# Reciprocal square roots of all norms: a logarithm and an exponential on ScalarE with one Newton step, in place of an integer shift with three

## The chip, the cores and the metric

The kernel runs on one core of one Trainium2 chip. The metric is the time of one execution on the device in microseconds (us), the median of several runs. In the profile PE is TensorE (matmul, PEld its weight loads), DVE is VectorE, ACT is ScalarE, POOL is GpSimd and SP the engine that issues most of the DMA transfers. Every engine works through its own queue of instructions in order, and waits on semaphores for the others.

## The reference

One decoder layer on 1024 tokens of width 1024, all in float32:

```python
x = layer_norm(x, ln_in_g, ln_in_b)
mix = hybrid_mixer(x, ...)        # 8 forgetting-attention heads, 4 HGRN2 heads
x = layer_norm(ALPHA * x + mix, ln_mix_g, ln_mix_b)
ffn = peer_ffn(x, ...)            # top-16 of 128^2 experts, 8 heads
x = layer_norm(ALPHA * x + ffn, ln_ffn_g, ln_ffn_b)
# layer_norm:     (x - mu) * rsqrt(var + 1e-5) * g + b        (over 1024 columns)
# head_rms_norm:   x * rsqrt(mean(x * x) + 1e-6) * g          (each head, in the mixer)
```

Both kinds of norm need a reciprocal square root of one number for each token (layer norm) or for each token and head (RMS norm of the mixer's outputs).

## The kernel before, in words

Tokens lie on the 128 partitions, in blocks of 128. The layer runs over three groups of tokens: 256, 512 and 256 (`GROUPS`). Each group goes through the input projection (`project_cols`), the mixer (`fox` and `hgrn`, two generators whose steps alternate), the output projection with the second layer norm (`mix_out`), the selection of experts (`select`, `select_tail`) and then the experts: four token blocks by gathering rows of the two tables (`gather_u`, `gather_v`, on POOL's DMA queue with the arithmetic on DVE or PE), the other four as a dense product with the whole tables (`dense`). Gathers and the building of the dense weights (`gbuild`) are cut into small pieces, which `tick` deals out between the steps of the other stages at hand-set rates. Only the pieces marked by `pin` keep the program's order; the rest of an engine's queue is put in order by the framework's scheduler, which works with its own estimates.

`rsqrt` (L221) is called in five places, 32 times in all, each time on a tile of 128 partitions and one to eight columns:

- `ln` (L250) from `first_ln`: four calls of two token blocks each, in the first projection.
- `hgrn` (L613): eight calls with four columns, one for each token block. What waits for the result is the scaling on ACT (L615), then POOL (L616) and the transposes on PE (L620).
- `fox` (L720): twelve calls with four or eight columns, one for each pair of heads in each group. What waits is the scaling on DVE (L722) and then the transposes (L727).
- `ln` from `mix_out`: three calls, one for each group, before the transposes L270 into the selection.
- `ln` from `finish`: four calls with one column, when a gathered block is done; and `finish_dense` (L1195), one call at the very end.

ACT is also the engine that evaluates Exp, Ln, Sigmoid, Silu and Gelu, and before some of these its queue holds an instruction `ACT_TABLE_LOAD`, which the compiler puts there. The softmax of `fox` (L679), the decays of `hgrn` (L514 to L550) and the copies of the transposed probabilities (L702) all run on ACT.

Of the kernel before, what the change touches and what calls it, by code (L numbers as in the profile page):

```python
# [12 lines left out]
I32 = mybir.dt.int32  # L13
U32 = mybir.dt.uint32
AF = mybir.ActivationFunctionType
ALU = mybir.AluOpType
# [4 lines left out]
P = 128  # L21
# [50 lines left out]
class Layer:  # L72
# [147 lines left out]

    def rsqrt(self, pool, x, n):  # L221
        V = self.nc.vector
        sh = pool.tile([P, n], U32, name="rssh", tag="rssh")
        y = pool.tile([P, n], F32, name="rsy", tag="rsy")
        t = pool.tile([P, n], F32, name="rst", tag="rst")
        V.tensor_scalar(sh, x.bitcast(U32), 1, None, op0=ALU.logical_shift_right)
        V.tensor_scalar(y.bitcast(I32), sh, -1.0, float(0x5F3759DF), op0=ALU.mult, op1=ALU.add)
        for _ in range(3):
            V.tensor_tensor(t, y, y, op=ALU.mult)
            V.scalar_tensor_tensor(t, t, -0.5, x, op0=ALU.mult, op1=ALU.mult)  # L230
            V.scalar_tensor_tensor(y, t, 1.5, y, op0=ALU.add, op1=ALU.mult)
        return y

    def ln_stats(self, st, n, x, halves=(0, 1)):
# [1067 lines left out]
```

## Time and profile before

| | |
|---|---|
| median of three runs | 3125.99 us (3123.66 to 3131.1) |
| the profiled execution | 3124.38 us, its span 3122.6 us |
| busy: PE, DVE, ACT, POOL | 2629.1, 2728.4, 1143.5, 1725.8 us |
| `ACT_TABLE_LOAD` on ACT | 29, each 1283 ns |

The span runs from the first instruction to the last; the execution is 1.8 us longer than the span. A row of a timeline gives the start, the duration, the engine, the line, the operation, output and inputs, and in brackets how long the engine had been idle and who ended that. Consecutive like instructions are merged (x2). A row of the waits gives the total, the number and the longest. By stage: the first group's mixer lies at about 90 to 200 us, the second's at 565 to 825, the third's at 1135 to 1270; the dense product with the remaining gathers takes from about 1500 to the end.

### The profile page before, as it was taken

Reading aid. Unit: us, or ns where it says so; the run is one execution under the profiler, and the core shown is the slowest. Engines: PE = TensorE matmul, PEld = TensorE weight load, DVE = VectorE, ACT = ScalarE, POOL = GpSimd, SP = SyncE. Lnnn points to the kernel's source line nnn. Section 1 sums busy time; section 2 is a strip of 40 time slices with the busy share of each in tenths; the row PEclk is TensorE's granted clock in tenths of the full one; section 3 lists DMA queues with packets and bytes.
Section 4 is the critical chain, followed back from the end, with each engine's and each line's share of the span. In section 5 each row is a group of like instructions: output and inputs, shape, how many; then the busy total and the mean of one; then the engine's idle time right before and its main releaser. Section 6 shows DMA issues by size and latency. Waiting matters only on the chain. (4 is left out here: it accounts for less than half of the span.)

```text
span 3122.6 us, 45664 instructions
## 1 busy us (share of the span) xinstructions
PE 2629.1 (84%) x16057; PEld 2161.1 (69%) x16057; DVE 2728.4 (87%) x5549; ACT 1143.5 (37%) x2028; POOL 1725.8 (55%) x1264
## 2 busy tenths in 40 slices
PE   7767799777779767767459899899999999999995
PEld 6767689656657445657347778787778877877874
DVE  8658766588769988989889899899999999999998
ACT  4733222455222433776523223232222323322321
POOL 2343477555756644654036666665467665656652
PEclk9879899888889889878779999999999999999997
DMA  7542599755968857663379999999999999999994
GB/s 272 191 143 81 195 353 318 224 157 169 336 247 297 282 192 268 221 232 149 149 243 366 333 380 359 350 362 367 345 362 371 380 379 357 356 375 337 371 338 159
DMA packets 338662, 887.13 MB, mean 284 GB/s; under 512 B 29912, under 2 KB 124136, under 8 KB 336000
## 3 DMA queue, kind: packets, MB, share of 16 engines
q0 software_dynamic: 147456, 536.94, 47.1%
q1 hardware_dynamic: 185200, 338.38, 31.1%
q10 hardware_dynamic: 5776, 8.90, 0.8%
q8 instruction: 126, 2.06, 0.3%
q14 instruction: 104, 0.85, 0.1%
HBM read 821.67 MB, written 62.42 MB: 283 GB/s over the span
## 5 line engine op out<-in xcount | busy, mean ns | idle before, releaser
L1090 POOL DMA_INDIRECT rows<-in_u,gsel x512 | 689.5, 1347 | 471.5 <-DVE rows L1109 291.7
L1090 POOL DMA_INDIRECT rows<-in_v,gsel x512 | 642.2, 1254 | 417.8 <-DVE ys L1134 261.2
L1109 DVE SCALAR_TENSOR_TENSOR rows<-rows,gx 128x1024 f32<-128x1024 f32 x512 | 633.2, 1285 | 37.9 <-DMA rows<-in_u,gsel 27.0
L1134 DVE SCALAR_TENSOR_TENSOR ys<-rows,sd,ys 128x1024 f32<-128x1024 f32 x381 | 489.7, 1285 | 0.6
L283 PE MATMUL psh<-dxh,uh 128*128 128x512 f32 x1024 | 402.8, 393 | 29.5 <-ACT uh L1016 16.5
L285 PE MATMUL psh<-dxh,ul 128*128 128x512 f32 x1024 | 401.0, 392 | 9.5 <-DVE ul L1017 9.4
L284 PE MATMUL psh<-dxl,uh 128*128 128x512 f32 x1024 | 400.5, 391 | 0.0
L284 PE MATMUL psf<-vl,hh 128*128 128x512 f32 x768 | 310.9, 405 | 44.0 <-DVE vl L1017 43.1
L1016 ACT ACTIVATE vh<-vr 128x512 fp32r<-128x512 f32 x256 | 161.8, 632 | 433.4 <-PE psv L285 402.7
L285 PE MATMUL psf<-vh,hl 128*128 128x512 f32 x768 | 305.8, 398 | 0.0
L283 PE MATMUL psf<-vh,hh 128*128 128x512 f32 x768 | 278.8, 395 | 9.3 <-DVE dy L1049 7.3
L1016 ACT ACTIVATE uh<-ur 128x1024 fp32r<-128x1024 f32 x128 | 136.0, 1062 | 406.2 <-PE psh L284 399.5
L283 PEld LDWEIGHTS psh<-dxh,uh 128*128 128x128 f32 x1024 | 193.5, 189 | 77.2 <-ACT hs L1030 20.5
L285 PEld LDWEIGHTS psh<-dxh,ul 128*128 128x128 f32 x1024 | 193.4, 189 | 50.5 <-DVE ul L1017 10.5
L210 ACT ACTIVATE whi<-wraw 128x1024 fp32r<-128x1024 f32 x130 | 136.5, 1056 | 241.9 <-PE psf L284 62.4
L213 POOL TENSOR_TENSOR wlo<-wraw,whi 128x1024 fp32r<-128x1024 f32 x70 | 172.8, 2474 | 91.7 <-ACT whi L210 89.2
L284 PEld LDWEIGHTS psh<-dxl,uh 128*128 128x128 f32 x1024 | 193.2, 189 | 39.5
L284 PEld LDWEIGHTS psf<-vl,hh 128*128 128x128 f32 x768 | 147.6, 192 | 91.4 <-DVE vl L1017 60.6
L1017 DVE TENSOR_TENSOR vl<-vr,vh 128x512 fp32r<-128x512 f32 x256 | 169.8, 685 | 12.4 <-ACT vh L1016 12.4
L283 PEld LDWEIGHTS psf<-vh,hh 128*128 128x128 f32 x768 | 145.4, 189 | 46.9 <-DVE dy L1049 9.6
L213 DVE TENSOR_TENSOR wlo<-wraw,whi 128x1024 fp32r<-128x1024 f32 x60 | 83.9, 1400 | 106.1 <-ACT whi L210 106.1
L285 PEld LDWEIGHTS psf<-vh,hl 128*128 128x128 f32 x768 | 148.1, 193 | 29.8
(338 smaller groups left out, 6510.4 us busy)
## 6 DMA issues: line engine op xcount, KB each, us to landing
ur<-in_ut SPq DMA_DIRECT2D x128, 512.0 KB
vr<-in_v SPq DMA_DIRECT2D x256, 256.0 KB
d_g<-slab SPq DMA_DIRECT2D x16, 2048.0 KB
gt<-d_g SPq DMA_DIRECT2D x32, 1024.0 KB
wraw<-in_wq SPq DMA_DIRECT2D x48, 512.0 KB
wraw<-in_wt SPq DMA_DIRECT2D x34, 512.0 KB
wraw<-in_wn SPq DMA_DIRECT2D x24, 512.0 KB
wraw<-in_wo SPq DMA_DIRECT2D x24, 512.0 KB
```

The lines of the kernel that those rows point to most:

```text
L210: nc.scalar.activation(hi, raw, AF.Copy)
L213: eng.tensor_tensor(lo, raw, hi.bitcast(F32), op=ALU.subtract)
L283: mm(out, lh, rh, start=start, stop=False, **kw)
L284: mm(out, lh, rl, start=False, stop=False, **kw)
L285: mm(out, ll, rh, start=False, stop=stop, **kw)
L1016: nc.scalar.activation(hi, raw, AF.Copy)
L1017: nc.vector.tensor_tensor(lo, raw, hi.bitcast(F32), op=ALU.subtract)
L1090: self.nc.gpsimd.indirect_dma_start(out=t, out_offset=None, in_=tab, in_offset=bass.IndirectOffsetOnAxis(ap=idx, axis=0))
L1109: self.pin(nc.vector.scalar_tensor_tensor(u, u, 1.0, x2, op0=ALU.mult, op1=ALU.mult, accum_out=sd[:, n : n + 1]), "u")
L1134: self.pin(nc.vector.scalar_tensor_tensor(ys, v, h, ys, op0=ALU.mult, op1=ALU.add), "w")
```

## The change

`rsqrt` takes its first estimate from ACT: the logarithm of x, written over by exp(-0.5 times it). One Newton step follows on DVE. Before, the estimate was made on DVE from the bits of x (a shift and a subtraction from a constant), and three Newton steps followed. The tile of the shift goes. The function has two lines less, so the lines of the kernel after it are lower by two in the changed kernel.

```diff
     def rsqrt(self, pool, x, n):
         V = self.nc.vector
-        sh = pool.tile([P, n], U32, name="rssh", tag="rssh")
         y = pool.tile([P, n], F32, name="rsy", tag="rsy")
         t = pool.tile([P, n], F32, name="rst", tag="rst")
-        V.tensor_scalar(sh, x.bitcast(U32), 1, None, op0=ALU.logical_shift_right)
-        V.tensor_scalar(y.bitcast(I32), sh, -1.0, float(0x5F3759DF), op0=ALU.mult, op1=ALU.add)
-        for _ in range(3):
-            V.tensor_tensor(t, y, y, op=ALU.mult)
-            V.scalar_tensor_tensor(t, t, -0.5, x, op0=ALU.mult, op1=ALU.mult)
-            V.scalar_tensor_tensor(y, t, 1.5, y, op0=ALU.add, op1=ALU.mult)
+        self.nc.scalar.activation(y, x, AF.Ln)
+        self.nc.scalar.activation(y, y, AF.Exp, scale=-0.5)
+        V.tensor_tensor(t, y, y, op=ALU.mult)
+        V.scalar_tensor_tensor(t, t, -0.5, x, op0=ALU.mult, op1=ALU.mult)
+        V.scalar_tensor_tensor(y, t, 1.5, y, op0=ALU.add, op1=ALU.mult)
         return y
```

In the changed kernel ACT's queue holds 92 table loads, 63 more than the 29 of before: 31 stand before a logarithm of `rsqrt` (L225) and 25 before its exponential (L226), the other seven are more before functions that were there already.

ACT's queue in the first group's mixer, where the first calls of `hgrn` and `fox` fall; `pr` are the softmax's exponentials, `pt` the transposed probabilities, E the decays, `ov` the scaling of HGRN2's output. Before:

```order
L550 ACTIVATE E<-E 128x512
L679 ACTIVATE pr,ls<-psf,nm 128x256
L702 ACTIVATE pt<-psf 128x256
L550 ACTIVATE E<-E 128x512
L702 ACTIVATE pt<-psf 128x128
L550 ACTIVATE E<-E 128x512
L679 ACTIVATE pr,ls<-psf,nm 128x128
L711 ACTIVATE o<-psv 128x2x64
L615 ACTIVATE ov<-ov,rsy 128x128 x4
```

The same place in the changed kernel:

```order
L225 ACT_TABLE_LOAD
L225 ACTIVATE rsy<-ms 128x4
L709 ACTIVATE o<-psv 128x2x64
L226 ACT_TABLE_LOAD
L226 ACTIVATE rsy<-rsy 128x4
L548 ACTIVATE E<-E 128x512
L677 ACTIVATE pr,ls<-psf,nm 128x256
L700 ACTIVATE pt<-psf 128x256
L225 ACT_TABLE_LOAD
L225 ACTIVATE rsy<-l_1622 128x4
L613 ACTIVATE ov<-ov,rsy 128x128
L226 ACT_TABLE_LOAD
```

Four table loads and four activations (the last Exp is the next row) now stand among the softmax, the decays and the copies.

ACT's queue in the dense product, where the second gathered block is finished (`rows` is its layer norm's scaling, `vh`, `uh` and `hh` the high parts of the tables' and the hidden tiles, `hs` the Gelu). Before:

```order
L1030 ACTIVATE hs<-psh 128x512
L1033 ACTIVATE hh<-hs 128x512
L1016 ACTIVATE vh<-vr 128x512 x2
L1016 ACTIVATE uh<-ur 128x1024
L1030 ACTIVATE hs<-psh 128x512
L259 ACTIVATE rows<-rows,lnnm,rsy 128x1024
```

The same place in the changed kernel:

```order
L1028 ACTIVATE hs<-psh 128x512
L1031 ACTIVATE hh<-hs 128x512
L225 ACT_TABLE_LOAD
L225 ACTIVATE rsy<-lnve 128x1
L1014 ACTIVATE vh<-vr 128x512
L226 ACT_TABLE_LOAD
L226 ACTIVATE rsy<-rsy 128x1
L1014 ACTIVATE vh<-vr 128x512
L257 ACTIVATE rows<-rows,lnnm,rsy 128x1024
L1014 ACTIVATE uh<-ur 128x1024
L1028 ACT_TABLE_LOAD
L1028 ACTIVATE hs<-psh 128x512
```

The logarithm and the exponential stand behind `hh` and one of them behind a `vh`, and the next Gelu has a table load of its own.

## Rows read from the trace of the kernel before

**Rows 1.** The page's first part: busy time, share of the span and number of instructions of each engine.

```profile
PE 2629.1 (84%) x16057; PEld 2161.1 (69%) x16057; DVE 2728.4 (87%) x5549; ACT 1143.5 (37%) x2028; POOL 1725.8 (55%) x1264
```

**Rows 2.** The busy time of each engine in the three mixers and in the last full stretch of the dense product; columns: from and to, length, PE, PEld, DVE, ACT and POOL busy, granted clock, share of the DMA engines, GB/s.

```profile
90.00:200.00 110.00, 78.18 (x856) 68.12 (x855) 74.62 (x176) 65.37 (x151) 38.39 (x36) 0.75 0.49 163
...
565.00:825.00 260.00, 191.49 (x1849) 144.67 (x1848) 193.74 (x434) 131.17 (x311) 151.02 (x130) 0.80 0.63 202
...
1135.00:1270.00 135.00, 103.96 (x1024) 69.53 (x1024) 108.76 (x401) 60.22 (x169) 63.27 (x62) 0.86 0.73 249
...
2300.00:3000.00 700.00, 674.22 (x2904) 546.09 (x2905) 689.33 (x893) 206.98 (x304) 449.08 (x334) 0.99 0.99 365
```

**Rows 3.** The timeline of DVE at the second layer norm of the second group, where nothing stands between the steps of `rsqrt`.

```profile
888.57 0.17 DVE L249 TENSOR_SCALAR lnve<-lnmv 128x4 f32<-128x4 f32 x1
888.77 0.17 DVE L226 TENSOR_SCALAR rssh<-lnve 128x4 uint32<-128x4 uint32 x1
888.98 0.17 DVE L227 TENSOR_SCALAR rsy<-rssh 128x4 int32<-128x4 uint32 x1
...
890.75 0.16 DVE L231 SCALAR_TENSOR_TENSOR rsy<-rst,rsy 128x4 f32<-128x4 f32 x1
```

**Rows 4.** The timeline of DVE in the first group's mixer: the first `hgrn` call, from 140.50 to 147.83, with three consecutive starts in the middle.

```profile
140.50 0.16 DVE L226 TENSOR_SCALAR rssh<-ms 128x4 uint32<-128x4 uint32 x1
...
144.18 0.15 DVE L226 TENSOR_SCALAR rssh<-l 128x4 uint32<-128x4 uint32 x1
144.25 0.15 DVE L229 TENSOR_TENSOR rst<-rsy 128x4 f32<-128x4 f32 x1
144.32 0.41 DVE L548 TENSOR_TENSOR E<-b 128x256 f32<-128x256 f32 x1
...
147.83 0.15 DVE L231 SCALAR_TENSOR_TENSOR rsy<-rst,rsy 128x4 f32<-128x4 f32 x1
```

**Rows 5.** The groups of instructions on ACT: one kind of table load and the smallest activation; count, busy us, mean ns, idle time before.

```profile
L509 ACT ACT_TABLE_LOAD x7 | 9.0, 1283 | 0.1
...
L522 ACT ACTIVATE eb<-b 128x4 f32<-128x4 f32 x8 | 1.6, 202 | 1.1 <-DVE b L511 1.0
```

**Rows 6.** The timeline of ACT around one table load in the first group's mixer.

```profile
120.21 0.60 ACT L482 ACTIVATE s<-psf 128x512 f32<-128x512 f32 x1
120.82 1.28 ACT L522 ACT_TABLE_LOAD   x1
122.11 0.21 ACT L522 ACTIVATE eb<-b 128x4 f32<-128x4 f32 x1
```

**Rows 7.** The waits of PE, and of ACT for PE, in the second group's mixer (565 to 825 us).

```profile
PE psv L704 <- ACT pt L702: 10.9, 18, 2.6
...
PE psf L701 <- ACT pr L679: 7.2, 5, 4.9
...
ACT pt L702 <- PE psf L701: 48.5, 28, 10.4
```

**Rows 8.** Who waited, in the whole span, for what reads or writes the tile `rsy`.

```profile
  PE psf L727: 25.4, 7
```

**Rows 9.** The timeline of DVE at the first layer norm.

```profile
8.08 0.16 DVE L249 TENSOR_SCALAR lnve<-lnmv 128x2 f32<-128x2 f32 x1
...
13.66 0.16 DVE L231 SCALAR_TENSOR_TENSOR rsy<-rst,rsy 128x2 f32<-128x2 f32 x1
```

**Rows 10.** The timeline of ACT there.

```profile
8.64 0.21 ACT L143 ACTIVATE lbe<-lbe 128x8 f32<-128x8 f32 x1
13.27 1.06 ACT L210 ACTIVATE whi<-wraw 128x1024 fp32r<-128x1024 f32 x1 [4.41 <-DMA wraw<-in_wt]
```

**Rows 11.** The timeline of DVE at the second layer norm of the first and of the third group.

```profile
227.09 0.16 DVE L249 TENSOR_SCALAR lnve<-lnmv 128x2 f32<-128x2 f32 x1
...
230.33 0.16 DVE L231 SCALAR_TENSOR_TENSOR rsy<-rst,rsy 128x2 f32<-128x2 f32 x1
...
1331.99 1.87 DVE L249 TENSOR_SCALAR lnve<-lnmv 128x2 f32<-128x2 f32 x1
...
1337.39 0.16 DVE L231 SCALAR_TENSOR_TENSOR rsy<-rst,rsy 128x2 f32<-128x2 f32 x1
```

**Rows 12.** The timeline of DVE where the second gathered block is finished.

```profile
2275.31 0.14 DVE L249 TENSOR_SCALAR lnve<-lnmv 128x1 f32<-128x1 f32 x1
...
2277.90 1.21 DVE L1109 SCALAR_TENSOR_TENSOR rows<-rows,gx 128x1024 f32<-128x1024 f32 x1
```

**Rows 13.** The timeline of ACT there.

```profile
2275.42 0.63 ACT L1033 ACTIVATE hh<-hs 128x512 fp32r<-128x512 f32 x1 [0.76 <-DVE hs L1032]
2276.07 0.63 ACT L1016 ACTIVATE vh<-vr 128x512 fp32r<-128x512 f32 x1
2278.80 0.63 ACT L1016 ACTIVATE vh<-vr 128x512 fp32r<-128x512 f32 x1 [2.10 <-PE psv L285]
```

**Rows 14.** The longest total in the list of waits of the whole span.

```profile
ACT vh L1016 <- PE psv L285: 402.7, 216, 13.6
```

**Rows 15.** The timeline of DVE at the last layer norm, `finish_dense`.

```profile
3105.56 0.16 DVE L1194 TENSOR_SCALAR lnve<-lnmv 128x4 f32<-128x4 f32 x1
...
3108.80 0.16 DVE L231 SCALAR_TENSOR_TENSOR rsy<-rst,rsy 128x4 f32<-128x4 f32 x1
```

## The prediction

> **What bounds the kernel now.** I read the busy time by engine first, then the stretches, then the waits and timelines around the calls. Over the span DVE is busy 87%, PE 84% and ACT only 37% [rows 1], so moving work from DVE to ACT looks free. By stretches it is not so simple. In the dense product, 2300 to 3000, PE and DVE are busy 674 and 689 of 700 us and the DMA engines 0.99 of the time [rows 2]: three resources are at their limit at once, and only five of the 32 calls fall behind the mixers and `mix_out`. Twenty calls fall in the three mixers (90 to 200, 565 to 825, 1135 to 1270), and there nobody is full: PE is busy 374, DVE 377 and ACT 257 of 505 us, which is 74%, 75% and 51% [rows 2]. These stages are chains that go round: PE makes logits, DVE takes a maximum, ACT an exponential, PE transposes, ACT copies, PE multiplies. PE waits for ACT's copies and exponentials (10.9 and 7.2 us of its 68.5 idle us in the second mixer), and ACT waits 48.5 us for PE's transposes [rows 7]. In such a loop an instruction put into any queue can be late for the others, although its engine is half idle. So the question is what ACT's additions do there, against what DVE is spared.
>
> **Removed.** Each call loses 8 of its 11 DVE instructions, 256 in all. Where nothing stands between, a step takes 0.2 us from start to start (888.77 to 888.98), though its duration is 0.16 to 0.17, since each needs the one before [rows 3]. Where other work is interleaved, it moves the next start by only 0.07 us (144.18, 144.25, 144.32) [rows 4]. So DVE gets back between 256 x 0.07 = 18 and 256 x 0.2 = 51 us, most of it at the low price, as the calls in the mixers are interleaved. It also gets a shorter chain: the first `hgrn` call needs from 140.50 to 147.98, 7.5 us, for what takes 2.2 us undisturbed (888.77 to 890.91) [rows 3, 4].
>
> **Added.** Each call adds two activations on ACT. The smallest that the trace shows takes 202 ns for four columns [rows 5]; I take 0.2 us, 64 x 0.2 = 13 us in all. The queue of the changed kernel holds 63 more table loads, at 1283 ns each [rows 5]: 81 us. Around one load nothing else is lost: the activation before it ends at 120.81, the load starts at 120.82 and the next activation at 122.11 [rows 6]. So the change puts 94 us on ACT and takes at most 51 from DVE. One call with both loads costs 2 x 1.28 + 2 x 0.2 = 2.97 us on ACT, one after the other, and three Newton steps at 0.2 behind it: 3.57 us from a finished variance to a finished root, against 2.2 on DVE alone.
>
> The Trainium skill, ScalarE: Activation LUTs, section What ACT_TABLE_LOAD costs, gives the load itself the same 1283 ns, but adds a drain of about 1380 ns to every switch. The row disagrees, with 1.30 us from one activation's end to the next one's start [rows 6]; by the page the additions would be 63 x 2.66 + 13 = 181 us and not 94. The same page (section Table sets: the hidden batching unit) says that a logarithm followed by an exponential needs one load, since one set holds both. The queue of the changed kernel has a load between them in 25 calls of 32; by that rule 25 x 1.28 = 32 us would go from the 94.
>
> **Where it meets the path.** Durations are those of the profiled execution (3124.38 us, 1.6 below the median).
>
> The first layer norm: the variance is ready at 8.24 and the last step ends at 13.82 [rows 9], since DVE does two long products in between. ACT is free from 8.85 until a weight arrives at 13.27 [rows 10], so the root comes at 8.85 + 3.57 = 12.42: 1.4 us earlier, and PE's first transposes wait for it. The three other calls of the first projection have slack, as the first group's matmuls run meanwhile: nothing.
>
> The three layer norms of `mix_out`, with PE waiting behind them. First group: ready at 227.25, root at 230.82 instead of 230.49, +0.3 [rows 11]; DVE's product in between hides the rest. Second: 888.74 + 3.57 = 892.31 instead of 890.91, +1.4 [rows 3]. Third: 1333.86 + 3.57 = 1337.43 instead of 1337.55, -0.1 [rows 11]. The last layer norm: 3105.72 + 3.57 = 3109.29 instead of 3108.96, +0.3 [rows 15]. With the start these five ends come to +0.5 us. That takes ACT to be free at each; if an Exp or a copy is in front of it, each is later by that.
>
> The mixers: of the 63 loads, 24 belong to the twelve calls elsewhere (4 + 3 + 4 + 1, two each) and two to Gelu, which leaves 37, or 47.5 us; with 40 activations, 8 us, that is 55.5 us on ACT in 505 us. The lower bound of what this costs is nothing (each falls in a gap), the upper all 55.5. An insert delays the next ACT instruction when ACT isn't waiting anyway, by its busy share 51%: 28 us. From that I take what DVE is spared, 20 x 8 x 0.07 = 11 us by its busy share 75%: 8. Of the remaining 20 I let half reach the end: ACT is late for PE in 18 of 68.5 idle us, a quarter, but PE's lateness comes back to ACT in the same loop. So +10 us. This is the term that decides, and it is the least certain.
>
> The gathered blocks in the dense product: DVE saves 8 x 0.07 = 0.6 us for each. ACT, in the new order, does `hh` (ends at 2276.05), load, logarithm, one `vh`, load, exponential. That `vh` waited for nothing in the trace (2276.07, while the next one waited 2.10 us for PE) [rows 13], so the estimate comes at 2276.05 + 2.97 + 0.63 = 2279.65. In its new order DVE has a `vl`, a `ul`, a `hl` and one gathered row before it needs the estimate, which it had done at 2279.1 [rows 12]: it stands 0.6 us. Saving and stand cancel. The two Gelu loads, 2.6 us, fall on an engine that waits for PE there (402.7 us in total for `vh`) [rows 14]: nothing.
>
> Sum: 0.5 + 10 + 0 = +10.5 us, on the median 3125.99 that is 3136.5, so 3137 us: slower by 0.35%. What a measurement of this kernel can tell from no change is about 0.2%, 6 us.
>
> **Rivals.** *The shorter chain wins* (faster). In the mixers a call's elapsed time falls from some 7.5 us to 3.6 plus what stands between, if ACT takes the logarithm at once. The price is bounded by what waits for it: PE's transposes L727 wait 25.4 us in seven places [rows 8]; with half of that, and the inserts all in gaps, it would be -12 us: 3114. For it: DVE stretches the chain worst where it is fullest. Against it: ACT's busy half, and that ACT's queue puts the calls behind copies which themselves wait for PE. Chance 0.2.
>
> *All hidden* (no change): ACT's gaps, 248 of 505 us in the mixers [rows 2], swallow every insert, and only the five ends remain: +0.5, 3126 to 3127. For it: the gaps are more than four times the inserts. Against it: they are cut into pieces of about 1.7 us (48.5 us over 28 waits) [rows 7], shorter than a call's 2.97. Chance 0.2.
>
> *Each switch drains ACT first*, so that it takes about twice the load: the mixers' 37 cost a further 37 x 1.28 = 47 us on ACT, by the same 51% and half +12, and the five ends, two loads each, +13: 3161. It is the mechanism of the page's drain, above. The one switch of rows 6 speaks against it. Chance 0.05.
>
> *DVE stands behind ACT in the dense product*: the estimate is behind a `vh` or `hh` that waits for PE, up to 13.6 us at the longest, 1.9 on average [rows 14]. With 5 us at three blocks, where DVE has no slack [rows 2], +15 on top of my sum: 3152. It decides from a wait of more than 0.6 us at that `vh`. Chance 0.05.
>
> **How the numbers follow.** My forecast, slower by 4 to 25 us with 3137 the likeliest, has 0.5. Slower by more than 0.2% gets that, less a little for its lower edge, and the two last rivals: 0.58. Within 0.2%: the second rival and the edges, 0.23. Faster: 0.19. The scheduler also puts other instructions in another order than before, and this can move either way what no row shows; I count it into the range. It reaches from a little below the first rival to the third: 3110 to 3161.
>
> **What would show it.** ACT's busy time should rise by about 94 us, to 1237, and DVE's fall by 30 to 50. If the mixers are the place, their three stretches together should be longer by about 10 us, with more PE time waiting for `pt` and `pr`; the dense product should be as long as before. The root of the last layer norm should come 3.6 us behind its variance. I am wrong if the mixers are no longer than before, if the waits of L727 shrink by more than 10 us, or if a wait of DVE for the exponential appears among the gathers.

## The result, and the profile after

The changed kernel takes 3167.99 us (3161.31 to 3171.29, 4 runs) beside 3128.55 us of the kernel before (3123.66 to 3132.01, 4 runs): ratio 1.0131 [1.0112, 1.0151], slower by 41 us [35, 47]. The sign was forecast; the forecast size, +10.5, is a quarter of what was measured, and 3168 lies above the range. The profiled execution took 3171.29 us.

The page of the changed kernel, first part, answers to [rows 1]:

```profile
PE 2640.1 (83%) x16057; PEld 2171.3 (69%) x16057; DVE 2694.1 (85%) x5293; ACT 1234.8 (39%) x2155; POOL 1721.5 (54%) x1264
```

ACT has 91 us more and DVE 34 less, as worked out (94, and 30 to 50). So the work was counted rightly and its price was not. The same four stretches as [rows 2], with the same columns (shifted by what the changed kernel is late there):

```profile
96.00:215.00 119.00, 81.27 (x862) 70.40 (x862) 65.05 (x129) 82.19 (x175) 38.62 (x37) 0.74 0.45 146
580.00:840.00 260.00, 189.07 (x1849) 144.00 (x1848) 184.20 (x368) 150.62 (x341) 149.31 (x130) 0.81 0.63 202
1153.00:1308.00 155.00, 110.03 (x1072) 76.34 (x1073) 110.66 (x372) 80.76 (x197) 68.50 (x66) 0.83 0.68 227
2350.00:3050.00 700.00, 675.60 (x2898) 546.28 (x2899) 678.78 (x867) 210.18 (x307) 437.57 (x328) 0.99 0.98 360
```

The first mixer is 9 us longer, the second not at all, the third some 20 (its borders fall among work that was reordered): 29 together, where some 10 were forecast. The steady dense product is unchanged. More exact is the lateness of the same matmuls, start in the changed kernel less start in the kernel before, median over those within 4 us of a place (worked out from the two traces, each of one execution; the other columns are the experiments of the first group, below):

| place in the kernel before, us | changed | e1 | e2 | e4 |
|---|---|---|---|---|
| 90, first projection done | +6.0 | -0.4 | -2.4 | -1.2 |
| 226, first mixer done | +14.6 | +5.1 | -9.8 | +4.5 |
| 565, second mixer begins | +15.0 | +7.3 | -8.6 | +6.3 |
| 825, second mixer done | +14.8 | +17.1 | -18.9 | +7.8 |
| 1080, third mixer ahead | +17.3 | +16.8 | -20.0 | +10.7 |
| 1330, third mixer done | +37.7 | +33.9 | -9.7 | +26.3 |
| 2280, before the second gathered finish | +39.3 | +42.1 | -8.9 | +26.3 |
| 2345, behind it | +48.7 | +42.8 | +1.0 | +27.1 |
| 3050 | +48.9 | +51.7 | +0.7 | +28.1 |

The loss thus has three kinds of place: the first projection (+6), two of the three mixers (+9, +20) and one step of +9 within 65 us around a gathered block. The loads, as groups of instructions of the changed kernel (they answer to [rows 5]):

```profile
L225 ACT ACT_TABLE_LOAD x31 | 39.8, 1283 | 0.9 <-ACT s L449 0.4
L226 ACT ACT_TABLE_LOAD x25 | 32.1, 1283 | 0.6 <-ACT rsy L225 0.2
```

The last column is what to read: ACT was idle 1.5 us in all in front of 56 loads, though it is idle 61% of the time. A load does not wait for the data of its activation (the last section has a row), so it starts as soon as ACT reaches it in its queue. Whether it is hidden shows behind it. Counted in the trace, in the three mixers (95 to 230, 560 to 870, 1080 to 1400) 53 of the 60 loads are followed by an activation within 0.1 us; seven are followed by a wait. ACT's timeline in the first mixer shows what that means:

```profile
190.34 0.55 ACT L700 ACTIVATE pt<-psf 128x256 f32<-128x256 f32 x2
190.91 1.28 ACT L225 ACT_TABLE_LOAD   x1
192.21 0.20 ACT L225 ACTIVATE rsy<-ms 128x4 f32<-128x4 f32 x1
192.43 1.28 ACT L226 ACT_TABLE_LOAD   x1
193.72 0.21 ACT L226 ACTIVATE rsy<-rsy 128x4 f32<-128x4 f32 x1
193.84 0.26 ACT L709 ACTIVATE o<-psv 128x128 f32<-128x128 f32 x1
194.70 0.69 ACT L613 ACTIVATE ov<-ov,rsy 128x128 f32<-128x128 f32 x2 [0.61 <-DVE rsy L229]
195.30 0.45 ACT L677 ACTIVATE pr<-psf,nm 128x256 f32<-128x256 f32 x1
195.66 0.19 ACT L677 ACTIVATION_READ_ACCUMULATOR pr<-psf,nm 128x1 f32 x1
195.86 1.28 ACT L225 ACT_TABLE_LOAD   x1
197.16 0.20 ACT L225 ACTIVATE rsy<-l 128x4 f32<-128x4 f32 x1
...
197.67 1.28 ACT L226 ACT_TABLE_LOAD   x1
198.97 0.20 ACT L226 ACTIVATE rsy<-rsy 128x4 f32<-128x4 f32 x1
199.08 0.39 ACT L613 ACTIVATE ov<-ov,rsy 128x128 f32<-128x128 f32 x1
199.37 0.36 ACT L700 ACTIVATE pt<-psf 128x256 f32<-128x256 f32 x1
```

And PE's in the same stretch:

```profile
195.90 0.69 PE L699 MATMUL psf<-ident,pr 128*128 128x128 f32 x2 [3.73 <-ACT pr L677]
199.78 1.22 PE L702 MATMUL psv<-v,pt 128*128 128x128 f32 x4 [3.20 <-ACT pt L700]
```

Of four loads in 8 us, two stand in front of `pr` and two in front of `pt`, and PE waits 3.73 and 3.20 us for just these two. Over the first mixer (90 to 245 us in both traces; total, number and longest) PE's waits for the two were, before:

```profile
PE psf L701 <- ACT pr L679: 6.9, 6, 2.2
...
PE psv L704 <- ACT pt L702: 2.5, 3, 1.7
```

and in the changed kernel:

```profile
PE psf L699 <- ACT pr L677: 12.5, 6, 5.1
...
PE psv L702 <- ACT pt L700: 7.8, 3, 4.3
```

In the stretches of the three mixers given above they add up to 38 us before and 61 in the changed kernel: 23 us more, of the 29 by which the mixers grew. DVE waits in front of the Newton step, too; of the waits for the tile `rsy`, which answer to [rows 8]:

```profile
  DVE rst L227: 40.4, 25
```

So two theories stand after the traces. *Loads*: each load delays whatever ACT has queued behind it, and the mixers wait for ACT. *Handoff*: DVE stands 40.4 us for the exponential at 25 calls, and what it does next is late. A third has no place of its own: *order*, since the scheduler puts at least 961 of PE's 16,057 matmuls elsewhere, and 313 of the 5197 instructions outside `rsqrt` that DVE has in both kernels (counted in the traces: the fewest that have to be moved to get the one order from the other).

### The profile page after: what moved, and what is told of

It reads as the page before. It is cut to its first block, busy times and chain, and to the rows that moved or that the text cites. A ratio compares the mean times of both kernels' runs of the same rounds, so it can differ in the third digit from the quotient of the medians.

```text
span 3169.5 us, 45511 instructions
## 1 busy us (share of the span) xinstructions
PE 2640.1 (83%) x16057; PEld 2171.3 (69%) x16057; DVE 2694.1 (85%) x5293; ACT 1234.8 (39%) x2155; POOL 1721.5 (54%) x1264
## 4 chain that ended last, share of the span: by engine, by line
PE 39%; DVE 36%; issue 9%; ACT 8%; DMA 4%; POOL 3%; SPq 0%; DVEq 0%; ACTq 0%; POOLq 0%
DVE ys L1132 7%; DVE rows L1107 6%; PE psf L282 6%; PE psf L283 6%; PE psf L281 5%; PE psh L283 4%; PE psh L281 4%; PE psh L282 4%; DVE dy L1047 2%; PE psv L702 1%; DVE vl L1015 1%; DVE tw L791 1%; DMA rows<-in_v,gsel 1%; DVE cand L831 1%; POOL rows L1088 1%
## 5 line engine op out<-in xcount | busy, mean ns | idle before, releaser
L283 PEld LDWEIGHTS psh<-dxh,ul 128*128 128x128 f32 x1024 | 193.3, 189 | 50.5 <-DVE ul L1015 10.5
L1015 DVE TENSOR_TENSOR ul<-ur,uh 128x1024 fp32r<-128x1024 f32 x128 | 156.6, 1224 | 18.0 <-ACT uh L1014 17.3
```

What stands on the lines that cost most here:

```text
L283: mm(out, ll, rh, start=False, stop=stop, **kw)
L1015: nc.vector.tensor_tensor(lo, raw, hi.bitcast(F32), op=ALU.subtract)
```

## The experiments

Four groups of four; each group ran on one chip beside runs of the kernel before, whose medians there were 3124.89, 3153.63, 3160.19 and 3160.68 us. So only ratios are compared, and us are the ratio applied to that median. "Loads" are those in the trace; the kernel before has 29, the changed one 92.

**e1, the loads without the wait.** Before's `rsqrt`, with this behind its last step:

```diff
+        z = sh.bitcast(F32)
+        self.nc.scalar.activation(z, x, AF.Ln)
+        self.nc.scalar.activation(z, z, AF.Exp, scale=-0.5)
         return y
```

> All 32 calls keep the three Newton steps of the kernel before, and ScalarE computes the logarithm and the exponential beside them into a tile that nobody reads; nothing is left out. If the table loads on ScalarE are the cause (some 63 loads, 81 us, that stand in front of copies and exponentials in the mixers and the first projection), it is slower than before by 30 to 45 us, as the changed kernel is. If the wait of VectorE for the exponential is the cause (40 us of waits in the changed kernel), it is slower by at most 10 us, since VectorE waits for nothing here. If the new order of the instructions is the cause, it is within 10 us of before, since the order is nearly the old one.

1.0122 [1.0090, 1.0153], +38 us, with 95 loads. The page's first part:

```profile
PE 2642.1 (83%) x16057; PEld 2171.4 (68%) x16057; DVE 2714.4 (86%) x5549; ACT 1236.7 (39%) x2158; POOL 1718.5 (54%) x1264
```

ACT as busy as in the changed kernel, DVE with all its 5549 instructions, nobody waiting for the result, nearly the old order (208 matmuls of PE differ): a loss of the whole size is there. The table above adds that it is made up otherwise: nothing in the first projection, 10 us in the second mixer. So in the first projection loads alone cost nothing; there the changed kernel loses by loads that DVE waits behind. In the second mixer, where the changed kernel loses nothing, the relief of DVE (e2 gains 10 us there) makes up for its loads.

**e2, the handoff without the loads; e3, the relief alone.**

```diff
-        for _ in range(3):
+        self.nc.scalar.activation(y, y, AF.Copy)   # e2 only
+        self.nc.scalar.activation(y, y, AF.Copy)   # e2 only
+        for _ in range(1):
```

> The first estimate comes from the shift and the subtraction on VectorE, goes through two Copy activations on ScalarE (which need no table) and gets one Newton step: two handoffs and no load; two Newton steps are left out, so the root is good to about 0.2%. If the table loads are the cause, it is within 8 us of before, or faster. If the handoffs themselves are, it keeps 15 us or more of the 40. If the new order is the cause, nothing can be said ahead: the order is a third one.

> Shift, subtraction and one Newton step, all on VectorE, as before but with two steps less (192 instructions); the root is good to about 0.2%. It shows what the relief of VectorE is worth without ScalarE. By the 0.07 us and the three quarters of my sum it is faster by 10 to 15 us; if the shorter chain wins in the mixers as the first rival had it, by 15 to 35; if the order that the scheduler makes from shorter chains is itself the cause of the loss, it is slower than before by 10 us or more.

e2: 0.9979 [0.9960, 0.9998], -7 us; e3: 0.9967 [0.9948, 0.9985], -10. A trip to ACT and back, with two activations there, costs about nothing; without loads in it DVE stands only 5.4 us for it, at ten calls. So the handoff by itself is not the cause, and neither is a new order as such: e3 is reordered nearly as much as the changed kernel (813 matmuls of PE) and wins. The long stands of the changed kernel, 40.4 us, are stands behind loads; only e1 shows that the loss comes without them. Yet in its trace e2 is 20 us ahead at 1080 and has nothing left at 3050: it loses 10 in the third mixer and another 10 between 2280 and 2345.

**e4 and e12, by place.** The new `rsqrt` beside the old one as `rsqrt_new`; in e4 `hgrn` and `fox` call it, in e12 `ln` (the last layer norm, `finish_dense`, keeps the old one in both).

> Only the 20 calls in the mixers have the new form; the 12 others are as before. If the mixers carry the loss: slower by 20 to 40 us. If it lies in the first projection and in the layer norms of mix_out: slower by 10 us at most. My sum gave the mixers +10.

> Only the 11 calls of the layer norms outside the mixers (four in the first projection, three in mix_out, four of the gathered blocks) have the new form: 52 loads, 23 more. If the places add up, it is slower by what the mixers' run left over, 41 - 28 = 13 us; my sum gave these calls nothing in the first projection and nothing in the gathered blocks, 0.2 in all.

e4: 1.0091 [1.0061, 1.0122], +28 us with 67 loads. e12: 1.0072 [1.0048, 1.0097], +23 with 52. The mixers carry most, as forecast, at nearly three times the size; the layer norms, which I had at next to nothing, carry the rest, and more than the 13 us expected of e12. The sum, 51, is more than the whole's 41, but the intervals (19 to 38 and 15 to 31 against 34 to 48) do not exclude that they add.

**e5 and e6, the table loaded by hand.** Before the first activation, in front of an exponential and a logarithm of the projection, and behind the stages with Sigmoid and Silu and the first Gelu; in e5 on the changed kernel (there also in front of the gathered and last layer norms), in e6 on the kernel before:

```diff
+        self.nc.scalar.preload_act_table_set("natural_log_exp_and_others")
...
+            self.pin(self.nc.scalar.preload_act_table_set("natural_log_exp_and_others"))
```

> The changed kernel with the same arithmetic, but the table that holds both logarithm and exponential is loaded by hand at the start and behind the stages that use Sigmoid, Silu and Gelu, so that most calls need no load: 24 loads in the queue instead of 92 (29 in the kernel before). If the loads are the cause, as the shadow run says (38 us for 63 loads, 0.6 us each), the 68 loads give back some 41 us: 3120 to 3132, or a little faster than before. If the logarithm and exponential themselves, their handoff or the new order carry part of it, it stays above 3140.

> The kernel before, with the old reciprocal square roots, and the common table loaded by hand in the same way: 13 loads instead of 29. At 0.6 us each it is faster than before by some 10 us; if a load in the mixers was hidden in the kernel before, it is the same.

The traces have 26 and 15 loads. e5: 0.9991 [0.9981, 1.0001], -3 us: the same instructions and 66 loads fewer than the changed kernel, and the 41 us are gone. Its page has ACT at 1151.0 us. A rival goes with them: that the logarithm, waiting for its data, holds up what ACT has queued behind it. ACT stands 75 us for that in the changed kernel and 80 in e1, but as long in e5 (79) and 104 in front of the copies of e2, and neither of these is slower than before. e6: 0.9999 [0.9986, 1.0012]: taking 14 loads from the kernel before gives nothing, where 10 us were expected. So the price was found for loads that were added, not for those that were there; why is open.

**e9 to e11, the dose.** e9 is the changed kernel unaltered; e10 loads the common table in front of each logarithm (the line of e5, in `rsqrt`, with the logarithm queued behind it); e11 is e1 with both activations written twice.

> The changed kernel itself, unaltered, beside the next three on one chip: 92 loads in the queue, 63 more than before, and 1.3% slower again, some 40 us.

> The changed kernel, with the table that holds both functions loaded by hand in front of each logarithm, so that the exponential behind it needs none: 61 loads in the queue, 32 more than before instead of 63, and the same arithmetic. If the time goes by the number of loads, the loss is halved: 20 us slower than before. If it goes by the calls (handoff, order, the activations), it stays at 35 to 40.

> The shadow run with logarithm and exponential computed twice into the unread tile: 157 loads in the queue, 128 more than before. If each load costs the same 0.6 us as in the single shadow, 76 us slower than before (2.4%); if the first ones fill ACT's gaps, more than that, up to 128 x 1.28 = 164; if later ones follow one another where the first already made PE wait, less than 60.

| run | loads more than before | ratio | us | us for one load |
|---|---|---|---|---|
| e10 | 32 | 1.0076 [1.0051, 1.0101] | +24 | 0.75 |
| e9 | 63 | 1.0130 [1.0107, 1.0152] | +41 | 0.65 |
| e1 | 66 | 1.0122 [1.0090, 1.0153] | +38 | 0.58 |
| e11 | 128 | 1.0305 [1.0283, 1.0328] | +96 | 0.75 |

The time goes by the number of loads, from half to twice the dose, at about half of their 1.28 us; twice the dose costs rather more than twice (96 us, where 0.6 us for each load gave 76). The last column is not a pure price: e9 and e10 also have DVE's relief and the gathered calls' loss (below), and in all four the activations are added, too. Kernels that differ in little but loads say the same: e10 has the same calls, steps and activations as e9, 31 loads less and 17 us less, 0.55 us for each; from e5 to e10 it is 27 us for 35 loads, 0.77.

**e7 and e8, two Newton steps on DVE**: `range(3)` becomes `range(2)`, e8 with the table of e6.

> The kernel before with two Newton steps instead of three (96 instructions of VectorE less): a root that is still good to some 5 parts in a million. By the run with one step, which won 0.33% for 192 instructions, half of that: 3 to 8 us faster.

> Both at once, two Newton steps on VectorE and the common table: 13 to 20 us faster than before if the two gains add; if both fall on the same waits, no more than 10.

Both came out otherwise than expected: 1.0013 [0.9998, 1.0028] and 1.0022 [1.0004, 1.0040], nothing won or a little lost. The traces have the pattern of e2: some 15 us ahead at 900 (e7), and a step of 13 us near 2300. All kernels with a shorter DVE chain in the gathered blocks have that step (e2, e3, e5, e7 to e10, e12 and the changed one); e4, e6 and e11, which keep the chain there, have 5 us of it at most, and e1, which keeps it too, 7 further on. That made the last group.

**e13 to e16, the gathered blocks.** `finish` sets a flag around its `ln`; in e13 only these four calls are new, in the others only they are old:

```diff
+        self.fin = 1
         self.ln(self.gp, [x2], [x2], g, b, ...
+        self.fin = 0
```

> Only the four calls in the layer norms of the gathered blocks have the new form; the queues differ from those of before only around these four places. If the jump of 10 to 13 us near 2300 belongs to the shorter chain there, it is slower by 10 to 13 us and the trace shows the step right behind the second call. If the jump comes from what earlier stages left behind (another phase of the weight stream), it is within 5 us of before. My prediction had these calls at nothing.

> The changed kernel, but with the old eleven steps in the four calls of the gathered blocks: 82 loads instead of 92. If the jump belongs to these calls, slower than before by some 30 us (1.0%) instead of 41; if not, by 38 to 41.

> Two Newton steps on VectorE everywhere but in the gathered blocks, which keep three: no load is added. If the jump belongs to these calls, 8 to 12 us faster than before, where the run with two steps everywhere was 0.1% slower; if not, the same as before.

> Logarithm and exponential with the common table loaded by hand, but the old eleven steps in the gathered blocks: 15 loads in the queue, 14 fewer than before. If the jump belongs to these calls, 12 to 16 us faster than before, and so faster than both kernels; if not, within 5 us of before, as the run with the common table was.

e13: 1.0041 [1.0026, 1.0055], +13 us for four calls. e14: 1.0068 [1.0054, 1.0082], +21, half of e9's loss and less than the 30 expected. e15: 0.9962 [0.9950, 0.9975], -12 us. e16: 0.9949 [0.9936, 0.9963], -16 us: the new estimate with its table kept loaded, and the old steps in the four gathered calls, is faster than both kernels. e13 has ten loads more than before as well, so it does not tell loads from order; e7 and e15 do: they differ in these four calls alone, neither adds a load, and one is 4 us slower than before, the other 12 faster.

How four calls cost 13 us is read from e13 around the second of them. DVE's timeline in e13 (the reads of accumulators left out):

```profile
2312.82 1.22 DVE L1123 SCALAR_TENSOR_TENSOR rows<-rows,gx 128x1024 f32<-128x1024 f32 x1
...
2314.76 0.16 DVE L228 TENSOR_TENSOR rst<-rsy 128x1 f32<-128x1 f32 x1 [0.71 <-ACT rsy L227]
...
2339.20 1.28 DVE L1063 TENSOR_TENSOR dy<-dy,psf 128x512 f32<-128x512 f32 x2
2340.40 0.68 DVE L1048 TENSOR_TENSOR hl<-hs,hh 128x512 fp32r<-128x512 f32 x1
2341.00 1.22 DVE L1123 SCALAR_TENSOR_TENSOR rows<-rows,gx 128x1024 f32<-128x1024 f32 x1
...
2345.58 1.22 DVE L1123 SCALAR_TENSOR_TENSOR rows<-rows,gx 128x1024 f32<-128x1024 f32 x1
...
2346.73 0.68 DVE L1063 TENSOR_TENSOR dy<-dy,psf 128x512 f32<-128x512 f32 x1
2347.33 0.68 DVE L1063 TENSOR_TENSOR dy<-dy,psv 128x512 f32<-128x512 f32 x1
...
2360.36 1.23 DVE L1031 TENSOR_TENSOR ul<-ur,uh 128x1024 fp32r<-128x1024 f32 x1 [4.45 <-DMA vr<-in_v]
```

and the wait of PE that answers to it:

```profile
2347.47 0.80 PE L297 MATMUL psf<-vh,hh 128*128 128x512 f32 x1 [6.14 <-DVE dy L1063]
```

In the kernel before, all four parts of `dy` stand in one piece:

```profile
2310.51 1.22 DVE L1109 SCALAR_TENSOR_TENSOR rows<-rows,gx 128x1024 f32<-128x1024 f32 x1
...
2311.66 1.87 DVE L1049 TENSOR_TENSOR dy<-dy,psf 128x512 f32<-128x512 f32 x3
2313.46 0.67 DVE L1049 TENSOR_TENSOR dy<-dy,psv 128x512 f32<-128x512 f32 x1
```

The wait for the exponential is 0.71 us, what I had estimated (0.6). As I read the rows, the price is in the order: in e13 five gathered rows stand between the second and third part of `dy`, PE waits 6.14 us for the third (and 3.29 us for `hh` at 2340), the splits of the weights come later, and the weight stream is late in turn (DVE waits 4.45 us for `vr`). The stretch, in the kernel before and then in e13 (columns as in [rows 2]):

```profile
2270.00:2345.00 75.00, 67.51 (x275) 53.73 (x274) 73.70 (x127) 20.29 (x29) 52.37 (x38) 0.93 0.99 362
```

```profile
2305.00:2390.00 85.00, 69.35 (x275) 53.94 (x274) 74.64 (x121) 24.55 (x34) 55.22 (x38) 0.90 0.91 325
```

The same 275 matmuls in 85 us instead of 75, with the DMA engines at 0.91 instead of 0.99. That the step goes with these four calls is shown by e13, e15 and e16, and that it needs no load by e7 beside e15. That the split `dy` is what decides among all that is reordered there was only read from the trace.

## Why the prediction was right or wrong

- *What is removed and added on each engine*: right (DVE -34, ACT +91). A load takes 1283 ns and nothing else around it: 190.91 to 192.21 is 1.30 us, as in [rows 6]. The rule of the Trainium skill that every switch to another table set adds a drain of about 1380 ns to the load (ScalarE: Activation LUTs, What ACT_TABLE_LOAD costs) thus does not hold here. That the drain rival's 3161 lies near the result is chance: the loss is the loads themselves. The other rule of the Trainium skill, that a logarithm and an exponential behind it need one load (same page, Table sets: the hidden batching unit), holds once the program asks for it: with the common set loaded by hand, e5 and e10 have no load between the two in 30 of 32 calls, and by e10 that is worth 17 us. What the prediction calls three Newton steps behind the exponential are the three instructions of the one step; its 3.57 us stand.
- *The mixers, +10*: right place and sign, wrong size; this is the step that failed. They measured +28 (e4) with the relief; without it, e1 is later by 5.5, 9.8 and 17.1 us over the three of them (the table's 226 less 90, 825 less 565, 1330 less 1080), 32 beside the 55.5 us of inserts. I had multiplied these by ACT's busy share, which left 28, taken 8 off for the relief, and then halved. The first two come out near what was measured: 28 beside 32, and e4 is later by 5.7, 1.5 and 15.6 us over the same places, 23 in all, 10 less than e1. The halving is what failed. It took half of ACT's delay to be lost on the way to the end; its ground, that ACT was late for PE in 18 of 68.5 idle us, tells how often PE waited for ACT before the change and not what comes of a later ACT, and in the traces PE's waits for `pt` and `pr` alone grow by 23 us. Without it the sum would have been some 20; with the two places that it put at nothing, the gathered calls (13) and the first projection (6), that is near the 41. The busy share may have come out by luck, too: it takes an insert to fall at random, and in the stretch shown it does not. There the scheduler puts load, logarithm and exponential between `pt` and `pr` of the loop, where ACT has just become the late one, while ACT's idle time sits at other places of its queue.
- *Three calls of the first projection, nothing*: wrong. The changed kernel is 6 us late at 90; e4, without these calls, is not. At 60.74 DVE waits 2.54 us for the exponential, and PE 2.84 us at 54.61 for the weight's low part `wlo`, which DVE makes; PE's waits for `wlo` in the first 90 us grow from 3.0 to 7.2. e1 (loads that DVE does not wait behind) and e2 (a trip to ACT without loads) are not late there, so it takes the two together.
- *Layer norms of `mix_out`, +0.3, +1.4 and -0.1*: the first two are borne out, +0.6 (226 to 300) and +1.4 (825 to 900) by the lateness of the matmuls; the third can't be told from the mixer ahead of it.
- *First layer norm, -1.4*: wrong sign, +0.4 (the last step ends at 14.18 instead of 13.82). ACT was not free: an older exponential stood in its queue and waited for data, so the logarithm ran late:

```profile
7.70 1.28 ACT L143 ACT_TABLE_LOAD   x1 [7.70 <-DMA lbl<-in_lbl]
10.33 0.21 ACT L143 ACTIVATE lbe<-lbe 128x8 f32<-128x8 f32 x1 [1.35 <-DVE lbe L142]
10.55 1.28 ACT L225 ACT_TABLE_LOAD   x1
11.85 0.20 ACT L225 ACTIVATE rsy<-lnve 128x2 f32<-128x2 f32 x1
```

- *Last layer norm, root 3.6 us behind its variance*: 2.35 us (3153.52 to 3155.87), since one of the two loads was already done:

```profile
3143.51 1.28 ACT L225 ACT_TABLE_LOAD   x1
3153.56 0.21 ACT L225 ACTIVATE rsy<-lnve 128x4 f32<-128x4 f32 x1 [8.76 <-DVE lnve L1192]
3153.78 1.28 ACT L226 ACT_TABLE_LOAD   x1
3155.08 0.21 ACT L226 ACTIVATE rsy<-rsy 128x4 f32<-128x4 f32 x1
```

- *Gathered blocks, nothing*: wrong by 13 us (e13), though the stand itself was sized rightly. I had only summed the durations; what the new order does to the work around them was put at nothing and left to the range.
- *Rivals*: the shorter chain is real, -7 to -10 us without loads (e2, e3) and -12 to -16 with the gathered calls left alone (e15, e16), but smaller than what the loads cost. "All hidden" falls with e1. "DVE stands behind ACT in the dense product" had the right stage for a part of the loss and the wrong reason: the stand is 0.71 us.

Left open: why e6 gains nothing from 14 loads taken away, why the part of the inserts that counts is so near ACT's busy share, and whether the places add up exactly.

## What to carry to other kernels

An engine's idle share says nothing of where an inserted instruction falls: look up what stands behind it in the queue, and where another engine waits for that, do not discount the delay a second time without a row that shows where it is lost. Here the added loads cost 0.58 to 0.75 us each of their 1.28, on an engine that was idle 61% of the time. Before a function is moved to ACT, count the table loads that it brings, and keep the set that holds all the functions of the stage loaded. Shortening a chain among interleaved work changes the order of that work; where the copying of results out of PE's accumulators (`dy`) or a stream of weights stands in it, compare their order before and after as well as the sum of durations.

## What the runs showed of the hardware

A table load does not wait with its activation: at 3143.51 it ran 10.05 us before the logarithm, which waited for its data until 3153.56, so this load, in front of a long wait, cost ACT nothing. (In the rows of the first layer norm the bracket behind the first load names the transfer of `lbl`; but DVE waited for `lbl` until 9.86, and the load had run at 7.70.) The kernel before differs by 1.1% between the four groups, each on a chip of its own (3124.89 to 3160.68), much of it in the third mixer: e13, on a chip where the kernel before takes 3160.68, has DVE and ACT do the same as in that kernel, in the same order, up to its first gathered finish near 1340; its matmuls are in time with the first trace up to 1100 (-1.6 us) and 27 us late at 1250. The ratio held all the same: the changed kernel has 1.0131 in the result and 1.0130 in e9. Comparing times across groups would have hidden every gain found here.
